# Products of two heads issued side by side on the column halves; the first attention's key remainder over 128 rows

## The chip, the cores and the metric

The program runs on one core of a Trainium2 chip. The metric is the device time of that core in microseconds (us), the median of several executions. Of the kernel before there are three: 2319.04, 2317.48 and 2319.41.

## The reference

Three transformer blocks follow each other on one sequence of 512 tokens with 1024 features, all in float32. The parts that the change touches, one in each block:

```python
# block 1: merged dilated attention, 8 heads of 64
s = jnp.einsum('bdhnqe,bdhnke->bdhnqk', qs, ks) * (E ** -0.5) + bias[None, None, :, None]
o = jnp.einsum('bdhnqk,bdhnke->bdhnqe', p, vs) / den
...
# block 2: attention, 8 heads, keys of 96, values of 64
s = jnp.einsum('bqhd,bkhd->bhqk', qi, k, preferred_element_type=jnp.float32) * scale
w = jax.nn.softmax(s, axis=-1).astype(v.dtype)
return jnp.einsum('bhqk,bkhd->bqhd', w, v)
...
# block 3: state space (SSD), 12 heads of 64, chunks of 128 tokens
cb = jnp.einsum('bclgn,bcsgn->bcgls', cc, bc)
y_diag = jnp.einsum('bcgls,bcghls,bcsghp->bclghp', cb, l_dec, xc)
y_off = jnp.einsum('bclgn,bcghpn,bcghl->bclghp', cc, prev, jnp.exp(a_cum))
```

Around them stand the projections of each block, a gated linear recurrence (block 1, after the attention), a long convolution (block 2), an mLSTM and a retention mixer (block 3), and two feed-forward layers.

## The kernel before

**Products.** A tile holds 128 features of all 512 tokens. A projection is a chain of products into one PSUM bank, three for each 128 rows of weights, since weights and activations are both split into a high and a low part (`acc_T`; the weights by L110 on ACT and L111 on DVE). Every product of the program is issued by `mm`, L116, so in the profile they all carry that line and are told apart by their tiles. A product named `128*64` in a row uses all 128 rows of TensorE's array and 64 of its columns: its result is 64 features of one head. Products whose operands are plain float32 go through the array in two passes, and a profile row counts passes (`x2` for one product); those of split parts take one.

**Banks.** The tiles of a tag go around a fixed number of banks: "mm" (projections) three, "s" (scores) two, "t" (transposes) two, "o" (values) one. A product into a tile waits until what the bank held before has been read.

**The order.** The program is written stage by stage, but the order on each engine is not the written one: a scheduler simulates the whole program (`schedule_with_timeline_sim=True`) and emits instructions by readiness and priority. Within an engine the emitted order is fixed; an instruction at the head that waits holds all behind it. Numbers behind a tile's name (mm_2236) count the tiles of the program as they are allocated, and order rows show them; profile rows leave them out.

**First attention** (`attn1`, four pairs of heads). A projected pair of q (or k) fills 128 partitions, 64 for each head. For head hh the tile q{hh} holds the high part of q in one half of its partitions and the low part in the other; k{hh} holds the high part of k in both. So one product over 128 rows gives q times the high part of k. The rest of k is `kl`: one tile for both heads, the half `kl[a]` for each, and its product with the high half of q uses 64 rows (`64*128` in a row). Each score block is written by these two products, 256 to 512 columns wide. DVE adds the bias and takes the maximum, ACT the exponential, POOL the division.

`values` goes through head 0 with its four blocks of keys, then head 1: for block j it transposes the 4 - j blocks of the probabilities p into a "t" bank (L599), copies them to SBUF (`pT`, two buffers, L604 on DVE for odd j, L606 on ACT for even), and multiplies v by pT, 512 - 128 j columns, into the 64 partitions of the head in bank "o". DVE's L609 (`of`) multiplies by the gate z, and ACT's L173 begins the split into the pair oa. Projections of the next pair and, after the last pair, of the recurrence stand between.

**Recurrence** (`hgrn`). For each head three projections, f, q and z, fill the three "mm" banks: L680 (`k`, tanh) and L681 (`b`, logarithm) read the first, L688 (`th`) the second, L693 (`th`) the third. Logarithms and tanh or exponentials need different tables, and ACT loads one at each switch (ACT_TABLE_LOAD). `decays` follows: differences `d` (POOL), their exponentials (ACT, L712), `qk` (DVE, L716), products `s<-qk` on TensorE, and `kd` (POOL, ACT, DVE, ending in L755), which is transposed at L760. Its tiles lie where those of the first attention were.

**Second attention** (eight heads). `scores` of a head gives four blocks P; `values(hd, ...)` transposes them (L1453), copies (`pT`, two buffers; L1456 on DVE for the last block, L1458 on ACT for the others) and multiplies, 512 columns each, into the head's half of "o". After block `SPREAD` = 1 of a second head the inverse row sums are spread over the partitions (`inverse_sums`). Output products of the convolution are held back to fill places in it.

**State space** (`Ssd`, called by `mix3`). For each of 12 heads, `decay` makes the decay factors (bank "o", DVE, ACT) and multiplies them with the shared products of B and C: `AD` inside the four chunks, `AO` between chunks, two buffers each. `values` then issues ten products of 128 columns into the head's half of "o", four of AD and six of AO, with `xd` (tokens times dt) as the other operand. The loop makes the decays of head hd + 1 before the values of head hd; a projection or two from `fill`, and the gate z of the next pair, stand between. `Retention` takes its AD and AO from the same pool.

At the end of block 1, eight tiles of x are loaded again by ACT's DMA queue (L840).

## Time and profile before

| | us |
| --- | --- |
| median of three executions | 2319.04 |
| span of the profiled execution | 2316.4 |
| TensorE (PE) busy in it | 2267.0 |
| DVE busy | 1389.2 |
| ACT busy | 941.6 |
| POOL busy | 537.1 |

The profiled execution is one of its own; the profile gives its span, and the time of the program lies around it. PE's rows show when a pass over the array starts and how long it lasted until its end; since passes are pipelined, one row's end overlaps the next one's start, and the pace is read from the starts. PEld is the loading of weights into the array, which runs beside it. In brackets behind a row stand the idle time before it and what ended that.

### The profile page before, as it was taken

How to read it: one execution, taken by the hardware profiler on the slowest of the kernel's cores; microseconds unless marked ns; L12 is line 12 of the kernel's file. 1: busy time of each engine (PE TensorE's matmuls, PEld its weight loads, DVE VectorE, ACT ScalarE, POOL GpSimd, SP SyncE). 2: the span in 40 equal slices, each digit the busy share in tenths (PEclk: the TensorE clock that was granted, in tenths of full speed). 3: DMA queues.
4: the chain of work that ended last, by engine and by line, in shares of the span. 5: the costliest groups of instructions: out<-in, count | busy, mean ns of one | idle time of the engine just before them, and what ended most of it. 6: DMA issues, size and time to landing. Idle time of an engine off the chain costs nothing.

```text
span 2316.4 us, 29278 instructions
## 1 busy us (share of the span) xinstructions
PE 2267.0 (98%) x11180; PEld 1837.4 (79%) x11180; DVE 1389.2 (60%) x2228; ACT 941.6 (41%) x1579; POOL 537.1 (23%) x457
## 2 busy tenths in 40 slices
PE   7899999999999999999999999999999999999998
PEld 3676798888888985678888887888887888888886
DVE  8754566663354597578637747876757665433333
ACT  4344455552243445644424424444444323322221
POOL 5232445541121135222101103000111211220220
PEclk7999999999999999999999999999999999999999
DMA  8542222124333342123232234212222322223222
GB/s 327 164 145 64 74 65 65 51 66 130 100 95 103 115 140 62 68 93 108 78 123 91 81 126 143 91 65 73 78 92 91 127 73 100 100 79 113 100 81 74
DMA packets 82163, 232.59 MB, mean 100 GB/s; under 512 B 10047, under 2 KB 10943, under 8 KB 82024
## 3 DMA queue, kind: packets, MB, share of 16 engines
q1 hardware_dynamic: 67208, 205.49, 26.9%
q10 hardware_dynamic: 14816, 25.25, 3.4%
q8 instruction: 88, 1.44, 0.2%
q14 instruction: 51, 0.42, 0.1%
HBM read 215.99 MB, written 15.22 MB: 100 GB/s over the span
## 4 chain that ended last, share of the span: by engine, by line
PE 57%; issue 2%; DVE 2%; ACT 1%; DMA 0%; POOL 0%; ACTq 0%; POOLq 0%; DVEq 0%
PE mm L116 48%; PE s L116 3%; PE o L116 3%; PE t L116 1%; PE t L1453 1%; DVE sg L1599 0%; DVE wl L111 0%; PE t L1422 0%; DMA x<-scr_x 0%; DVE x L2267 0%; DVE x L1600 0%; ACT P L1439 0%; ACT wh L110 0%; PE t L1953 0%; ACT A L182 0%
## 5 line engine op out<-in xcount | busy, mean ns | idle before, releaser
L116 PE MATMUL mm<-A,wh 128*128 128x512 f32 (+1 forms) x2192 | 692.6, 392 | 1.0 <-DVE A L183 1.0
L110 ACT CAST wh<-wr 128x1024 fp32r<-128x1024 f32 (+3 forms) x370 | 363.5, 984 | 653.9 <-PE mm L116 463.5
L111 DVE TENSOR_TENSOR wl<-wr,wh 128x1024 fp32r<-128x1024 f32 (+3 forms) x366 | 437.7, 1197 | 296.2 <-ACT wh L110 294.4
L116 PE MATMUL mm<-B,wh 128*128 128x512 f32 x1688 | 541.9, 397 | 3.2 <-DVE B L183 1.9
L116 PEld LDWEIGHTS mm<-A,wh 128*128 128x128 f32 (+1 forms) x2192 | 408.9, 187 | 88.2 <-DVE A L183 1.8
L116 PE MATMUL mm<-A,wl 128*128 128x512 f32 (+1 forms) x1096 | 429.0, 392 | 0.5 <-DVE wl L111 0.5
L116 PEld LDWEIGHTS mm<-B,wh 128*128 128x128 f32 x1688 | 316.4, 188 | 73.9 <-DVE B L183 2.9
L116 PE MATMUL mm<-B,wl 128*128 128x512 f32 x844 | 332.4, 394 | 0.1
L116 PEld LDWEIGHTS mm<-A,wl 128*128 128x128 f32 (+1 forms) x1096 | 205.2, 187 | 43.4 <-DVE wl L111 0.9
L116 PEld LDWEIGHTS mm<-B,wl 128*128 128x128 f32 x844 | 159.0, 188 | 34.5 <-issue 1.5
L116 PE MATMUL mm<-a,wh 128*128 128x512 f32 x448 | 140.4, 389 | 0.0
L222 POOL TENSOR_TENSOR r<-r,mhalf 128x4 f32<-128x4 f32 (+1 forms) x40 | 53.7, 1344 | 350.9 <-DVE r L221 350.9
L239 DVE TENSOR_TENSOR us<-mm,bc 128x512 f32<-128x512 f32 x95 | 65.2, 689 | 99.8 <-PE mm L116 99.0
L175 POOL TENSOR_TENSOR a<-sl,a 128x512 fp32r<-128x512 f32 x28 | 40.5, 1446 | 274.2 <-ACT a L173 274.2
L116 PEld LDWEIGHTS mm<-a,wh 128*128 128x128 f32 x448 | 84.1, 188 | 17.4
L116 PE MATMUL mm<-a,wl 128*128 128x512 f32 x224 | 86.8, 389 | 0.0
L116 PE MATMUL mm<-wh,A 128*128 128x256 f32 x448 | 85.4, 287 | 0.0
L116 PEld LDWEIGHTS mm<-wh,A 128*128 128x128 f32 x448 | 71.6, 193 | 2.4 <-issue 1.0
L2187 POOL TENSOR_TENSOR sl<-sl,bc 128x512 f32<-128x512 f32 x22 | 28.7, 1305 | 167.6 <-DVE sl L1545 167.6
L116 PE MATMUL mm<-wl,A 128*128 128x256 f32 x224 | 64.2, 287 | 1.0 <-DVE wl L111 1.0
L712 ACT ACTIVATE d<-d 128x512 f32<-128x512 f32 x56 | 35.2, 629 | 69.7 <-POOL d L711 69.7
L116 PE MATMUL mm<-wh,B 128*128 128x256 f32 x320 | 61.0, 288 | 0.0
(583 smaller groups left out, 3597.1 us busy)
## 6 DMA issues: line engine op xcount, KB each, us to landing
wr<-w2upg SPq DMA_DIRECT2D x22, 512.0 KB, 3.4
wr<-w2upu SPq DMA_DIRECT2D x22, 512.0 KB, 3.5
wr<-w3fg SPq DMA_DIRECT2D x22, 512.0 KB, 3.4
wr<-w3fu SPq DMA_DIRECT2D x22, 512.0 KB, 3.4
adar<-w1ada SPq DMA_DIRECT2D x32, 256.0 KB, 5.1
wr<-w3out SPq DMA_DIRECT2D x16, 512.0 KB, 3.4
wr<-w2uh SPq DMA_DIRECT2D x12, 512.0 KB, 3.6
wr<-w2dn SPq DMA_DIRECT2D x16, 384.0 KB, 2.9
```

The costliest lines, as they stand in the source:

```text
L110: nc.scalar.copy(out=hi[:, :n], in_=r[:, :n])
L111: (eng or nc.vector).tensor_tensor(out=lo[:, :n], in0=r[:, :n], in1=hi[:, :n].bitcast(F32), op=ALU.subtract)
L116: self.nc.tensor.matmul(out, a, b, start=start, stop=stop)
L175: eng.tensor_tensor(out=l[:p], in0=src, in1=hi[:p].bitcast(F32), op=ALU.subtract)
L222: nc.gpsimd.tensor_tensor(out=r, in0=r, in1=self.mhalf[:, :n], op=ALU.pow)
L239: self.nc.vector.tensor_tensor(out=out, in0=ps, in1=bc, op=ALU.mult)
L712: nc.scalar.activation(out=d, in_=d, func=AF.Exp)
L1453: nc.tensor.transpose(ps[:, i * P : (i + 1) * P], pt[i][:, j * P : (j + 1) * P], k.ident)
L2187: nc.gpsimd.tensor_tensor(out=s, in0=s, in1=norm.bc, op=ALU.mult)
```

## The change

- `mm` returns its instruction. A new method `together` issues a list of products at high priority, so that nothing comes between them, and makes the first depend on all the copies that the list needs.
- First attention: the remainder of k lies in two persistent tiles, kl0 and kl1, each zeroed once (POOL) and filled in its head's half, and the remainder product goes over all 128 rows. `values` has the blocks j outside and the two heads inside: both heads' transposes and copies (head 0's on ACT, head 1's on DVE, four pT buffers), then their two products by `together`.
- Second attention: the transposes and the copy of a block become `turn`, with six pT buffers. The first head of a pair makes its four pT and keeps them; the second head works in two groups, each of two blocks: its two turns, then four products, first and second head in turn, by `together`. The inverse sums come after the first group.
- State space: AD and AO have four buffers. `values` takes a pair and issues its 20 products in one list, the two heads in turn, after the last operation of both decays. The loop of `mix3` goes by pairs, with the decays of both heads of the next pair and its z ahead of the values.
- Two small tiles (lb, pss) are allocated wider than they are used, `dynamic_dma_scratch_size=2048` is given to the program, and comments are gone.

```diff
     def mm(self, out, a, b, start, stop):
-        self.nc.tensor.matmul(out, a, b, start=start, stop=stop)
+        return self.nc.tensor.matmul(out, a, b, start=start, stop=stop)
+
+    def together(self, mms, after):
+        info = mybir.DependencyInfo(mybir.DependencyClass.Sync, mybir.DependencyReason.DATA)
+        with self.tc.high_priority():
+            for i, args in enumerate(mms):
+                m = self.mm(*args)
+                if i == 0:
+                    for a in after:
+                        self.tc.add_manual_dep(m.ins, a.ins.name, info, reason="issued in a row")
...
 def attn1(k, h, tab, oa, op):
+        kls = [p.tile([P, T], F32R, tag=f"kl{hh}", name=f"kl{hh}") for hh in range(2)]
+        for t in kls:
+            nc.gpsimd.memset(t.bitcast(F32), 0.0)
...
-            kl = p.tile([P, T], F32R, tag="kl", bufs=1, name=k.name("kl"))
             for hh, (a, b) in enumerate(rows):
+                kl = kls[hh]
...
-                ks.append((kt, kl[a]))
+                ks.append((kt, kl))
...
-                    k.mm(ps[:, :m], q[hh][a, i * P : (i + 1) * P], kp[hh][1][:, :m], False, True)
+                    k.mm(ps[:, :m], q[hh][:, i * P : (i + 1) * P], kp[hh][1][:, :m], False, True)
...
             po = k.bank("o", 1)
-            for hh in range(2):
-                pt, off = pts[hh]
-                c0 = (pr % 2) * P + hh * 64
-                for j in range(NT):
-                    n = T - P * j
+            for j in range(NT):
+                n = T - P * j
+                es, ready = [], []
+                for hh in range(2):
+                    pt, off = pts[hh]
...
-                    e = p.tile([P, T], F32, tag="pT", bufs=2, name=k.name("pT"))
-                    if j % 2:
-                        nc.vector.tensor_copy(out=e[:, :n], in_=ps[:, :n])
+                    e = p.tile([P, T], F32, tag="pT", bufs=4, name=k.name("pT"))
+                    if hh:
+                        ready.append(nc.vector.tensor_copy(out=e[:, :n], in_=ps[:, :n]))
                     else:
-                        nc.scalar.copy(out=e[:, :n], in_=ps[:, :n])
-                    k.mm(po[hh * 64 : hh * 64 + 64, j * P :], v[:, j, c0 : c0 + 64], e[:, :n], j == 0, j == NT - 1)
+                        ready.append(nc.scalar.copy(out=e[:, :n], in_=ps[:, :n]))
+                    es.append(e)
+                mms = []
+                for hh, e in enumerate(es):
+                    c0 = (pr % 2) * P + hh * 64
+                    mms.append(
+                        (po[hh * 64 : hh * 64 + 64, j * P :], v[:, j, c0 : c0 + 64], e[:, :n], j == 0, j == NT - 1)
+                    )
+                k.together(mms, ready)
...
+            def turn(pt, j):
+                ps = k.bank("t", 2)
+                for i in range(NT):
+                    nc.tensor.transpose(ps[:, i * P : (i + 1) * P], pt[i][:, j * P : (j + 1) * P], k.ident)
+                e = pd.tile([P, T], F32, tag="pT", bufs=6, name=k.name("pT"))
+                return e, V.tensor_copy(out=e, in_=ps) if j == 3 else S.copy(out=e, in_=ps)
+
+            first = []
+
             def values(hd, pt, po, den):
                 hh = hd % 2
-                for j in range(NT):
...
-                    k.mm(po[hh * 64 : hh * 64 + 64], v[:, j, hd], e, j == 0, j == NT - 1)
-                    if hh and j == SPREAD:
+                if not hh:
+                    first[:] = [turn(pt, j) for j in range(NT)]
+                    return
+                for j0 in (0, 2):
+                    es = [(first[j], turn(pt, j)) for j in (j0, j0 + 1)]
+                    k.together(
+                        [
+                            (po[a * 64 : a * 64 + 64], v[:, j, hd - 1 + a], e[a][0], j == 0, j == NT - 1)
+                            for j, e in zip((j0, j0 + 1), es) for a in range(2)
+                        ],
+                        [e[a][1] for e in es for a in range(2)],
+                    )
+                    if j0 == 0:
                         rows = inverse_sums(den)
...
-        AD = pool.tile([P, NT, P], F32, tag="AD", bufs=2, name=k.name("AD"))
-        AO = pool.tile([P, 768], F32, tag="AO", bufs=2, name=k.name("AO"))
+        AD = pool.tile([P, NT, P], F32, tag="AD", bufs=4, name=k.name("AD"))
+        AO = pool.tile([P, 768], F32, tag="AO", bufs=4, name=k.name("AO"))
...
-    def values(self, hd, AD, AO, po):
+    def values(self, pr, As, po):
         k, xd = self.k, self.xd
-        hh = hd % 2
-        out = po[hh * 64 : hh * 64 + 64]
+        mms = []
         for c in range(NT):
             sl = slice(c * P, (c + 1) * P)
-            for a in range(c):
-                o = OFF[a, c]
-                k.mm(out[:, sl], xd[:, a, hd * 64 : hd * 64 + 64], AO[:, o : o + P], a == 0, False)
-            k.mm(out[:, sl], xd[:, c, hd * 64 : hd * 64 + 64], AD[:, c], c == 0, True)
+            for a in range(c + 1):
+                for hh, (AD, AO, _) in enumerate(As):
+                    x = xd[:, a, pr * P + hh * 64 : pr * P + hh * 64 + 64]
+                    d = AD[:, c] if a == c else AO[:, OFF[a, c] : OFF[a, c] + P]
+                    mms.append((po[hh * 64 : hh * 64 + 64, sl], x, d, a == 0, a == c))
+        k.together(mms, [A[2] for A in As])
...
-                A = s.decay(0)
-                po = None
-                for hd in range(12):
-                    if hd % 2 == 0:
-                        po, z = k.bank("o", 1), zn
-                    fill.pop(0)()
-                    nx = s.decay(hd + 1) if hd < 11 else None
-                    s.values(hd, *A, po)
-                    A = nx
-                    if hd % 2:
-                        s.end(hd // 2, po, z)
-                    elif hd < 10:
-                        zn = s.z(hd // 2 + 1)
+                As = [s.decay(0), s.decay(1)]
+                for pr in range(6):
+                    po, z = k.bank("o", 1), zn
+                    nx = []
+                    for j in range(2):
+                        fill.pop(0)()
+                        if pr < 5:
+                            nx.append(s.decay(2 * pr + 2 + j))
+                    if pr < 5:
+                        zn = s.z(pr + 1)
+                    s.values(pr, As, po)
+                    As = nx
+                    s.end(pr, po, z)
```

Where this moves instructions, in the order that each kernel's build gives. First TensorE in the state space of before, at the last products of a pair: AD_12667 and AO_12668 are the first head's decays, AD_12751 and AO_12752 the second's, and o_12701 is their bank.

```order
L116 MATMUL o_12701<-AD_12667,xd 64x128
L116 MATMUL o_12701<-AO_12668,xd 64x128 x3
L116 MATMUL o_12701<-AD_12667,xd 64x128
L116 MATMUL o_12701<-AD_12751,xd 64x128
L116 MATMUL o_12701<-AO_12752,xd 64x128
L116 MATMUL o_12701<-AD_12751,xd 64x128
L116 MATMUL o_12701<-AO_12752,xd 64x128 x2
```

And of the change, at the first products of a pair (AD_12432 and AO_12433 belong to the first head, AD_12454 and AO_12455 to the second; mm_12995 is a projection):

```order
L116 MATMUL mm_12995<-wh_13004,B_11862 128x256
L116 MATMUL o_12474<-AD_12432,xd 64x128
L116 MATMUL o_12474<-AD_12454,xd 64x128
L116 MATMUL o_12474<-AO_12433,xd 64x128
L116 MATMUL o_12474<-AO_12455,xd 64x128
L116 MATMUL o_12474<-AD_12432,xd 64x128
L116 MATMUL o_12474<-AD_12454,xd 64x128
```

Before, each head's ten products stood together and the second head's followed the first's; now the two alternate.

Next TensorE at the end of the first attention, where the last products by values (o_1975, pT) stand among the projections of the recurrence's first head (mm_2164 f, mm_2201 q, mm_2236 z; mm_2392 is f of its second head). Before:

```order
L116 MATMUL mm_2236<-A_605,wh_2239 128x512
L116 MATMUL mm_2236<-A_605,wl_2240 128x512
L116 MATMUL mm_2236<-A_606,wh_2239 128x512
L116 MATMUL o_1975<-pT_2020,v_1395 64x256
L116 MATMUL o_1975<-pT_2025,v_1395 64x128
L116 MATMUL mm_2236<-A_609,wh_2239 128x512
L116 MATMUL mm_2236<-A_609,wl_2240 128x512
```

Of the change:

```order
L116 MATMUL o_1975<-pT_1988,v_1396 64x512
L612 MATMUL t_2006<-ident,p_1849 128x128 x2
L116 MATMUL o_1975<-pT_1996,v_1396 64x384
L116 MATMUL o_1975<-pT_2002,v_1396 64x384
L612 MATMUL t_2011<-ident,p_1892 128x128 x2
L612 MATMUL t_2018<-ident,p_1849 128x128
L612 MATMUL t_2022<-ident,p_1892 128x128
L116 MATMUL o_1975<-pT_2009,v_1396 64x256
L116 MATMUL o_1975<-pT_2014,v_1396 64x256
L116 MATMUL o_1975<-pT_2020,v_1396 64x128
L116 MATMUL o_1975<-pT_2024,v_1396 64x128
L116 MATMUL mm_2392<-A_601,wh_2395 128x512
```

Before, 18 products of mm_2236 follow the last product by values, then 24 of mm_2392, 24 of mm_2429 and 2 of mm_2464, and then the recurrence's first s<-qk. In the change all of mm_2236 comes earlier; the 24 of mm_2392 and 6 of mm_2429 stand between the last product by values and that s<-qk.

Last ACT at the same boundary, where the recurrence starts (k_2195, th_2232, b_2196 and th_2267 are of its first head, k_2423 of its second). Before:

```order
L680 ACTIVATE k_2195<-mm_2164 128x512
L688 ACTIVATE th_2232<-mm_2201 128x512
L110 CAST wh_2467<-wr_2465 128x1024
L681 ACT_TABLE_LOAD
L681 ACTIVATE b_2196<-k_2195,lb 128x512
L693 ACT_TABLE_LOAD
L693 ACTIVATE th_2267<-mm_2236 128x512
```

Of the change, whose lines stand 22 further down:

```order
L702 ACTIVATE k_2195<-mm_2164 128x512
L710 ACTIVATE th_2232<-mm_2201 128x512
L862 DMA x_4687<-xT 128x512
L862 DMA x_4689<-xT 128x512
L703 ACT_TABLE_LOAD
L703 ACTIVATE b_2196<-k_2195,lb 128x512
L862 DMA x_4691<-xT 128x512
L862 DMA x_4693<-xT 128x512
L715 ACT_TABLE_LOAD
L715 ACTIVATE th_2267<-mm_2236 128x512
```

The loads of x, which the program of before issues much later, now stand among the recurrence's first operations on ACT, and a cast of wh no longer stands ahead of the first logarithm.

## The prediction

> **What bounds the kernel now.** I read the page's busy shares first, then its chain, then the busy time in the stretches that the change touches.

> ```profile
> span 2316.4 us, 29278 instructions
> PE 2267.0 (98%) x11180; PEld 1837.4 (79%) x11180; DVE 1389.2 (60%) x2228; ACT 941.6 (41%) x1579; POOL 537.1 (23%) x457
> PE 57%; issue 2%; DVE 2%; ACT 1%; DMA 0%; POOL 0%; ACTq 0%; POOLq 0%; DVEq 0%
> 118.00:256.80 138.80, 138.80 (x677) 99.26 (x676) 67.16 (x189) 57.89 (x123) 34.88 (x32) 1.00 0.31 96
> 876.00:918.00 42.00, 39.24 (x169) 20.52 (x170) 35.65 (x51) 28.09 (x60) 26.30 (x18) 1.00 0.21 63
> 1500.00:1650.00 150.00, 150.00 (x929) 127.89 (x928) 106.36 (x231) 67.66 (x147) 11.27 (x6) 1.00 0.21 71
> ```

> TensorE (PE) is busy 98% of the span, and no other engine has more than 2% of the chain. The stretches (columns: length, then busy PE, PEld, DVE, ACT, POOL, then clock and DMA) are first attention, the front third of second attention, and the state-space heads. In the first and last PE never rests and DVE has 48% and 71%: a microsecond taken off PE there is a microsecond off the span, until PE is made to wait. The middle one differs: DVE is at 85%.

> **What the products cost now.** The products by values and state-space heads write 64 partitions each. Their PE time, by stretch:

> ```profile
> 118.00:256.80 138.80, 22.31 (x64) 1.00 0.31 96
> 870.00:1000.00 130.00, 34.09 (x64) 1.00 0.22 69
> 1480.00:1660.00 180.00, 26.39 (x240) 1.00 0.21 71
> ```

> Together 82.8 us. Each product is two passes over the array (64 passes for the 32 products of either attention). What one costs alone, with its borders, stands in the timeline (start, length):

> ```profile
> 906.46 0.39 PE L116 MATMUL s<-kT,qT 96*128 96x512 f32 x1
> 906.78 1.07 PE L116 MATMUL o<-pT,v 128*64 128x512 f32 x2
> 907.78 0.66 PE L1453 MATMUL t<-ident,P 128*128 128x128 f32 x4
> ...
> 1617.98 0.39 PE L116 MATMUL mm<-B,wl 128*128 128x512 f32 x1
> 1618.21 0.39 PE L116 MATMUL mm<-B,wh 128*128 128x512 f32 x1
> 1618.52 0.43 PE L116 MATMUL o<-AD,xd 128*64 128x128 f32 x2
> ...
> 1622.65 0.50 PE L116 MATMUL mm<-B,wh 128*128 128x512 f32 x1
> ```

> Lengths overlap, so I read starts. A projection follows the next after 0.23; the first 128*64 product comes 0.31 after one, so changing the shape of the array costs about 0.09 going in, and as much going out. Of the 1.00 from 906.78 to 907.78, two passes take 0.43 each (512 columns at 1.2 per ns), a first weight load 0.05, and the way out 0.09. So a run of these products costs 0.24 plus its passes. The 40 passes of this state-space pair take 4.13; but for the accident shown next they start 0.109 apart (128 columns at the same rate).

> **Do two halves run at once?** The program of before has one accident that answers this: where the second head of a state-space pair follows the first without a break.

> ```profile
> 1548.31 0.71 PE L116 MATMUL o<-AO,xd 128*64 128x128 f32 x5
> 1548.75 0.32 PE L116 MATMUL o<-AD,xd 128*64 128x128 f32 x1
> 1548.85 0.27 PE L116 MATMUL o<-AO,xd 128*64 128x128 f32 x1
> 1548.91 0.32 PE L116 MATMUL o<-AD,xd 128*64 128x128 f32 x2
> 1549.02 0.27 PE L116 MATMUL o<-AO,xd 128*64 128x128 f32 x1
> 1549.07 0.27 PE L116 MATMUL o<-AD,xd 128*64 128x128 f32 x1
> 1549.13 0.27 PE L116 MATMUL o<-AO,xd 128*64 128x128 f32 x1
> ```

> From 1548.85 to 1549.13 six passes start, 0.055 apart: twice the usual pace. By the order of before (first fence of the section on the change) the first head still had AO and AD passes to go when the AD of the second began at 1548.75. So the second half of the array takes work past waiting work of the first, and two heads issued in turn should take half. For 512 columns no row shows it; the bounds are no overlap and 2x, and I take 2x: a projection moves 512 columns in 0.23, so two of these passes in 0.43 ask no more columns per ns than that.

> [...]

> **Gains, term by term.**
> - First attention: 16 runs of one pair (4 pairs of heads, 4 blocks). Passes of a pair side by side: 2 x (0.43 + 0.32 + 0.21 + 0.11) = 2.13, with 4 x 0.24 = 3.1; four pairs 12.4, from 22.3: **9.9**.
> - Second attention: 8 runs of two pairs, 0.24 + 4 x 0.43 = 1.96 each, 15.7 from 34.1: **18.4**.
> - State space: 6 runs of 40 passes, 0.24 + 40 x 0.0545 = 2.4 each, 14.5 from 26.4: **11.9**.
> - The remainder of the keys (kl) over 128 rows:

> ```profile
> 174.22 0.36 PE L116 MATMUL s<-k,q 128*128 128x256 f32 x1
> 174.52 0.38 PE L116 MATMUL s<-kl,q 64*128 64x256 f32 x1
> 174.83 0.38 PE L116 MATMUL s<-k,q 128*128 128x256 f32 x1
> 175.14 0.38 PE L116 MATMUL s<-kl,q 64*128 64x256 f32 x1
> 175.45 0.50 PE L116 MATMUL mm<-A,wh 128*128 128x512 f32 x1
> ```

> Four products of 256 columns take 1.23, 0.31 each; at the projections' pace they need 0.12 each, 0.48. The difference, 0.75, is the change of shape at both borders of each kl, and with 128 rows it goes. 32 kl products, two to a group: 16 x 0.75 = **12.0**, with 0 as the other end, should the shape not be what costs it.

> Sum of gains **52.2**.

> **What comes late.** (a) The end of first attention. In the order of before 18 projections of mm_2236 stand behind the last product by values, and 50 more before the first s<-qk of the recurrence; in the new order none of mm_2236, 30 in all. The recurrence starts only when first attention is over, since ACT's k follows its cast of oa:

> ```profile
> 255.99 0.86 PE L116 MATMUL o<-pT,v 128*64 128x256 f32 x4
> 256.96 0.68 DVE L609 SCALAR_TENSOR_TENSOR of<-o,z 128x512 f32<-128x512 f32 x1
> ...
> 260.14 0.60 ACT L680 ACTIVATE k<-mm 128x512 f32<-128x512 f32 x1 [1.84 <-DVE hog L803]
> ...
> 269.68 0.58 ACT L680 ACTIVATE k<-mm 128x512 f32<-128x512 f32 x1
> ...
> 273.86 1.28 ACT L712 ACT_TABLE_LOAD   x1
> ...
> 277.23 0.96 DVE L755 TENSOR_TENSOR kd<-kd,k 128x384 f32<-128x384 f32 x1
> 274.67 1.10 PE L116 MATMUL s<-qk 128*128 128x64 f32 x8 [0.41 <-DVE qk L716]
> 278.25 0.55 PE L760 MATMUL t<-ident,kd 128*128 128x128 f32 x3 [1.49 <-DVE kd L755]
> ```

> With F for the start of DVE's of (256.96), k ends at F + 3.8 and kd at F + 21.2. Of the three "mm" banks mm_2164, mm_2201 and mm_2236 hold all, and mm_2392 needs the one that k empties: PE, done with the values at F - 0.1, now waits 3.9 there. Up to the transposes of kd it has 30 projections (6.8) and 8 small products (1.1), so it could be there at F + 7.8 without the wait, or F + 11.7 with it. When is kd ready? In the new order ACT does kd's inputs ahead of the next head's k, a logarithm, a cast and two table loads (269.68 to 275.14 in before): with one d (0.63) of that stretch still needed, 4.8 earlier, F + 16.4. Against that six x loads now stand in ACT's queue there, eight of which took 4.02 to issue (last row of the next fence) beside its operations; I add 0.9. So kd is ready at F + 17.3, and PE waits 9.5 in all, where before had 0.41 + 1.49: **7.6 lost**. Bounds: 3.9, the bank alone, and 11.5, kd at F + 21.2.

> (b) The last two blocks there have their transposes, copies and products back to back; a copy takes 0.59 on ACT:

> ```profile
> L1458 ACT COPY pT<-t x24: 559/586/595, 877.2 to 991.0; 128x512 f32<-128x512 f32 x24
> L116 PE MATMUL o<-pT,v 128*64 128x512 f32 x27 | 14.6, 618 | 0.4 <-ACT pT L1458 0.4
> 286.00:290.00 4.00, 4.00 (x22) 3.91 (x23) 3.93 (x11) 1.77 (x4) 2.60 (x4) 0.61 0.00 0
> 520.40 4.02 ACTq L840 DMA_DIRECT2D x<-xT  x8
> ```

> Two to three copies in the open: **1.3** (0 to 2.8). Everywhere else of the two attentions several projections or score products stand between the last transpose and the run that needs it, more than a copy.

> (c) Front of second attention: its 27 passes (second row) are 13.5 products, 14.7 us with borders, which become 13.5 / 4 x 1.96 = 6.6. PE would need 42 - 8.1 = 33.9, less than DVE's 35.65. With DVE at 95% the stretch takes 37.5, so **3.6 lost** (1.8 to 6).

> (d) The clock: the waits at 274 to 286 were followed by a stretch at half clock (0.61 from 286 to 290, third row). More idle time may bring another: **1.0** (0 to 1.7). (e) Small waits at other runs, of which the 27 passes had 0.4 (second row of the last fence): **1.4** (0 to 5).

> At nothing: two memsets on POOL (23% busy); copies shifted from ACT to DVE (DVE half idle there); the eight x loads, which leave 520 (last row) for the recurrence's start, beyond what (a) holds, as issues run beside ACT's operations; 19 weight loads on SP that follow the moved z products, four buffers ahead with DMA at 21%. If that cover fails, a late load costs PE its delay once.

> Losses 14.9, net **37.3**. The profiled span 2316.4 becomes 2279.1; the median of the runs, 2319.04, is 2.6 longer than that span, so the time is **2281.7**.

> **Rivals.**
> 1. Nearly all the gain arrives: kd early, DVE's work shifted behind the front third, losses 5: 2272. For it: PE is 100% busy in two of the three stretches. Chance 20%.
> 2. Strict order: a half starts only behind the passes issued earlier. Then a pair takes 3 slots for 2, two pairs 5 for 4, 40 passes 21 for 20: gains 5.6 + 15.0 + 11.2 + 12.0 = 43.8, less 14.9: 2290. Against it, the AD at 1548.75 went past waiting passes; for it, no row has 512 columns. Chance 12%. [...]
> 3. No overlap (the change doesn't do what it says): only borders are saved, 1.3 + 4.7 - 1.2, and kl, 16.8 in all; losses (a) and (b) 8.9, while (c) goes: 2311. The passes 0.055 apart speak against it. Chance 5%. [...]
> 4. Slower: a run waits for the copies of both heads, and all of PE's queue waits behind it. There are 24 such runs in the attentions. If the last copy comes d after PE arrives, the kernel loses 24 d + 8.9 against 52.2: break-even at d = 1.8, three copies of 0.59; at four copies, 2.4, it is 14 slower, 2333. Against it: the projections between, named in (b). Chance 3%.
> 5. My forecast, waits between 10 and 20: 2277 to 2287. Chance 60%.

> So faster by over 0.2% (about what a measurement of this kernel can tell from no change) 0.95, within it 0.02, slower 0.03. The range holds rivals 1 and 2 and the bounds of the losses, and leaves out 3 and 4: 2268 to 2296.

> **What would show it.** The products by values and state space at 12, 16 and 15 us of PE time by stretch; two starts within 0.1 of each other in each run; kl as 128*128 starting 0.12 to 0.23 after its k; PE idle for 4 at the first mm after first attention and for some 6 more up to the transposes of kd; DVE near 95% in the front of second attention. Wrong would be: 512-column passes of the two halves 0.43 apart, or new waits of over 20 in sum.

## The result

Four executions of the changed kernel took 2282.62 us in the median (2279.68 to 2287.6), four of before beside them 2319.22: a ratio of 0.9844, 95% interval 0.9825 to 0.9863. The forecast was 2281.7. (Of the runs below one execution, in experiment 4, took 2767.35 at a granted clock of 0.748; it is left out of that median.) The page of the profiled execution (whole span, busy time of the engines, chain that ended last):

```profile
span 2278.5 us, 29275 instructions
PE 2216.6 (97%) x11180; PEld 1822.6 (80%) x11180; DVE 1391.8 (61%) x2228; ACT 939.0 (41%) x1579; POOL 534.1 (23%) x459
PE 56%; DVE 2%; issue 2%; ACT 1%; POOL 0%; POOLq 0%; DVEq 0%; ACTq 0%
```

TensorE is busy 50.4 us less and idle 61.9 us of the span instead of 49.4, 12.5 more. Where that happened is seen by cutting both spans at the same instructions: the first s<-k of first attention, the last transposes of kd in the recurrence, the second wait at the start of the feed-forward layer of block 2, and the last transposes of the program. Busy time by such a stage (columns: length, then busy PE, PEld, DVE, ACT, POOL, clock, DMA), before:

```profile
109.49:498.31 388.82, 384.50 (x2219) 316.25 (x2218) 238.75 (x482) 193.10 (x357) 166.82 (x184) 1.00 0.25 78
498.31:1027.50 529.19, 521.37 (x2539) 407.09 (x2537) 306.18 (x435) 230.23 (x397) 136.55 (x107) 1.00 0.32 101
1027.50:2306.76 1279.26, 1273.56 (x6087) 1056.58 (x6087) 752.91 (x1198) 470.82 (x753) 188.71 (x130) 1.00 0.28 93
```

and after:

```profile
109.46:481.42 371.96, 362.86 (x2218) 310.93 (x2217) 239.05 (x483) 191.51 (x357) 166.74 (x184) 0.99 0.28 87
481.42:1001.57 520.15, 504.60 (x2539) 408.80 (x2537) 307.62 (x434) 229.57 (x397) 135.76 (x107) 0.99 0.31 99
1001.57:2268.75 1267.18, 1261.38 (x6086) 1045.19 (x6087) 754.21 (x1198) 470.41 (x753) 186.12 (x130) 1.00 0.29 94
```

The stage of first attention and recurrence is 16.9 shorter, that of second attention 9.0, the rest with the state space 12.1. Length less busy time is TensorE's idle time: 4.3 became 9.1, 7.8 became 15.6, and in the rest it stayed at 5.7 to 5.8.

What the products that write one half of the columns cost, by the same view as before (PE busy in them, first attention, second attention, state space):

```profile
104.80:241.10 136.30, 11.95 (x64) 1.00 0.41 126
868.00:994.00 126.00, 15.82 (x64) 0.96 0.25 82
1480.00:1620.00 140.00, 14.43 (x240) 1.00 0.23 76
```

So 10.4, 18.3 and 12.0 less, against 9.9, 18.4 and 11.9 in the forecast. Four products of the scores in first attention, and one run of a pair there, on the timeline (start, length):

```profile
109.46 0.28 PE L116 MATMUL s<-k,q 128*128 128x256 f32 x1
109.58 0.28 PE L116 MATMUL s<-kl,q 128*128 128x256 f32 x1
109.70 0.28 PE L116 MATMUL s<-k,q 128*128 128x256 f32 x1
109.82 0.28 PE L116 MATMUL s<-kl,q 128*128 128x256 f32 x1
109.94 0.40 PE L116 MATMUL mm<-A,wh 128*128 128x512 f32 x1
...
148.53 1.08 PE L116 MATMUL o<-pT,v 128*64 128x512 f32 x4
149.54 0.66 PE L612 MATMUL t<-ident,p 128*128 128x128 f32 x4
```

Four passes of 512 columns take 1.01 with their borders (148.53 to 149.54), where two took 1.00: both halves run at once. By the trace the four start at 148.53, 148.54, 149.01 and 149.02. The four score products take 0.48, as forecast, instead of 1.23.

The end of first attention, on the timeline (the last column is the idle time before and its releaser). F, the start of DVE's of, is 241.07:

```profile
241.07 0.69 DVE L630 SCALAR_TENSOR_TENSOR of<-o,z 128x512 f32<-128x512 f32 x1 [0.54 <-PE o L116]
...
244.85 0.80 PE L116 MATMUL mm<-A,wh 128*128 128x512 f32 x1 [3.82 <-ACT k L702]
...
256.67 0.58 DVE L777 TENSOR_TENSOR kd<-kd,k 128x384 f32<-128x384 f32 x1 [0.31 <-ACT kd L776]
257.30 0.55 PE L782 MATMUL t<-ident,kd 128*128 128x128 f32 x3 [1.67 <-DVE kd L777]
```

The wait for k's bank came as forecast, 3.8. kd was ready at F + 16.2, and TensorE waited 1.7 for it. In second attention the waits (engine, line, releaser: us, times, longest) are led by

```profile
PE s L116 <- ACT P L1461: 6.3, 6, 3.3
```

and the longest of them has this on DVE:

```profile
879.16 0.67 DVE L1389 TENSOR_TENSOR tmp<-tmp,tmp 128x512 f32<-128x512 f32 x1
...
882.65 1.77 DVE L193 SCALAR_TENSOR_TENSOR B<-ya,vec,B 128x512 fp32r<-128x512 f32 x1
884.34 1.75 DVE L1389 TENSOR_TENSOR tmp<-tmp,tmp 128x512 f32<-128x512 f32 x1
886.01 1.27 DVE L1459 TENSOR_REDUCE st<-s 128x1 f32<-128x512 f32 x2
...
887.56 0.79 PE L116 MATMUL s<-kT,qT 96*128 96x512 f32 x1 [3.34 <-ACT P L1461]
```

The maxima st of two score blocks, whose last products started between 882.17 and 883.18, stand in DVE's order behind work of the convolution (L1389) and the split of the attention's own output (B); ACT's exponential P follows st, and TensorE needs the bank that P empties.

### The profile page after: what moved, and what is told of

Read it like the earlier page. It is cut to its first block, busy times and chain, and to the rows that moved or that the text cites. A ratio compares the mean times of both kernels' runs of the same rounds, so it can differ in the third digit from the quotient of the medians.

```text
span 2278.5 us, 29275 instructions
## 1 busy us (share of the span) xinstructions
PE 2216.6 (97%) x11180; PEld 1822.6 (80%) x11180; DVE 1391.8 (61%) x2228; ACT 939.0 (41%) x1579; POOL 534.1 (23%) x459
## 4 chain that ended last, share of the span: by engine, by line
PE 56%; DVE 2%; issue 2%; ACT 1%; POOL 0%; POOLq 0%; DVEq 0%; ACTq 0%
PE mm L116 49%; PE s L116 3%; PE o L116 2%; PE t L116 1%; DVE sg L1634 0%; PE t L1474 0%; ACT wh L110 0%; DVE wl L111 0%; DVE x L2304 0%; DVE B L193 0%; DVE x L1635 0%; DVE st L1459 0%; PE t L1989 0%; ACT A L192 0%; PE t L1952 0%
## 5 line engine op out<-in xcount | busy, mean ns | idle before, releaser
L116 PE MATMUL mm<-A,wh 128*128 128x512 f32 (+1 forms) x2192 | 693.2, 392 | 4.8 <-ACT k L702 3.8
L111 DVE TENSOR_TENSOR wl<-wr,wh 128x1024 fp32r<-128x1024 f32 (+3 forms) x366 | 438.0, 1198 | 282.4 <-ACT wh L110 280.4
L116 PE MATMUL mm<-B,wh 128*128 128x512 f32 x1688 | 541.9, 397 | 3.6 <-DVE B L193 2.1
L116 PEld LDWEIGHTS mm<-A,wh 128*128 128x128 f32 (+1 forms) x2192 | 409.8, 188 | 91.0 <-ACT k L702 4.1
L116 PE MATMUL mm<-A,wl 128*128 128x512 f32 (+1 forms) x1096 | 430.1, 393 | 1.1 <-DVE wl L111 1.1
L116 PEld LDWEIGHTS mm<-B,wh 128*128 128x128 f32 x1688 | 316.6, 188 | 75.4 <-DVE B L193 3.7
L116 PE MATMUL mm<-B,wl 128*128 128x512 f32 x844 | 332.4, 394 | 0.0
L116 PEld LDWEIGHTS mm<-A,wl 128*128 128x128 f32 (+1 forms) x1096 | 206.0, 188 | 44.0 <-DVE wl L111 1.9
L116 PEld LDWEIGHTS mm<-B,wl 128*128 128x128 f32 x844 | 159.0, 188 | 34.0 <-issue 1.2
L116 PE MATMUL mm<-a,wh 128*128 128x512 f32 x448 | 140.4, 389 | 0.0
L116 PEld LDWEIGHTS mm<-a,wh 128*128 128x128 f32 x448 | 84.1, 188 | 17.4
L116 PE MATMUL mm<-a,wl 128*128 128x512 f32 x224 | 86.8, 389 | 0.0
L116 PE MATMUL mm<-wh,A 128*128 128x256 f32 x448 | 84.6, 285 | 0.0
L116 PEld LDWEIGHTS mm<-wh,A 128*128 128x128 f32 x448 | 70.7, 191 | 1.1 <-issue 0.6
L116 PE MATMUL mm<-wl,A 128*128 128x256 f32 x224 | 63.7, 285 | 1.0 <-DVE wl L111 1.0
L1609 DVE TENSOR_TENSOR x<-x,mm 128x512 f32<-128x512 f32 x32 | 22.0, 687 | 64.5 <-PE mm L116 64.5
```

The lines of the kernel that those rows point to most:

```text
L111: (eng or nc.vector).tensor_tensor(out=lo[:, :n], in0=r[:, :n], in1=hi[:, :n].bitcast(F32), op=ALU.subtract)
L116: return self.nc.tensor.matmul(out, a, b, start=start, stop=stop)
L1609: k.nc.vector.tensor_tensor(out=xs[n], in0=xs[n], in1=ps, op=ALU.add)
```

## The experiments

All but the first change the changed kernel; times are medians, stages as above.

**1. The remainder of the keys alone, in the kernel before.**

```diff
+        kls = [p.tile([P, T], F32R, tag=f"kl{hh}", name=f"kl{hh}") for hh in range(2)]
...
-                    k.mm(ps[:, :m], q[hh][a, i * P : (i + 1) * P], kp[hh][1][:, :m], False, True)
+                    k.mm(ps[:, :m], q[hh][:, i * P : (i + 1) * P], kp[hh][1][:, :m], False, True)
```

> The kernel before with the remainder of the keys over 128 rows alone (two zeroed tiles, nothing else of the change). Theory (the change of the array's shape at both borders is what the 64-row products cost): each of the 32 costs its columns alone, 0.12 for 256, and the time falls by 10 to 12, to 2307 to 2309; TensorE's order at the end of first attention stays that of before, so no wait of 3.9 for a bank appears there. Rival (they cost it by something else): 0, 2319.

The two tiles are zeroed once; the edit also has the change's `dynamic_dma_scratch_size`. Measured 2308.94 against 2319.84, ratio 0.9957 (0.9942 to 0.9972): 10.9 less, the theory's time. Its first stage, and a row in it that before does not have:

```profile
108.73:490.91 382.18, 374.21 (x2219) 315.62 (x2218) 238.47 (x483) 193.04 (x357) 167.96 (x184) 0.99 0.28 86
```

```profile
118.65 0.50 PE L116 MATMUL mm<-A,wl 128*128 128x512 f32 x1 [3.60 <-DVE wl L111]
```

TensorE is busy 10.3 less (384.50 less 374.21), although it ran 3.4 us more at half clock than before (the mean granted clock is 0.99 in this row and 1.00 in that of before), and in this execution 3.6 of the gain were handed to a new wait: the low part of a weight, made by DVE, is late. It is in the changed kernel too (0.5 in its profile). Experiments 7 and 10 follow it.

**2. How far past waiting passes a pass can start.** Inside a run, the heads change after g products instead of after each:

```diff
+        hs = mms[0::2], mms[1::2]
+        mms = [m for c in range(0, len(hs[0]), g) for h in hs for m in h[c : c + g]]
```

> The changed kernel with the products inside a run grouped by head, nothing else: the six state-space pairs change heads after 1, 2, 3, 4, 5 and 10 products of a head (10 is head after head); in second attention pairs 1 and 3 change after every product, pairs 2 and 4 after two. It tells how far a pass may stand behind waiting ones and still start on the free half. In the kernel before, head after head, 40 passes cost 4.22 with borders where 40 x 0.109 + 0.24 would be 4.60, so 3.4 passes were saved at the one change of heads. Theory (a pass starts when its half is free and it is among the 4 oldest that have not started): 2.42, 2.53, 2.75, 3.18, 3.62 and 4.27 us for the six pairs; in second attention 1.96 alternating and 2.39 by twos. Rival (a depth of 8 or more): 2.42, 2.42, 2.42, 2.53, 2.75, 3.84, and 1.96 for both. Rival (the two halves need the two products next to each other): 2.42, 3.5, 3.8 and more. TensorE never rests around the state space, so the time grows by the sum of the differences: theory 4.4 + 0.9 = some 5 us, to 2287.

The six state-space pairs (length of the window, PE busy in their 40 passes), for g = 1, 2, 3, 4, 5 and 10:

```profile
1509.00:1513.00 4.00, 2.40 (x40) 1.00 0.00 0
1531.00:1535.00 4.00, 2.45 (x40) 1.00 0.01 4
1550.00:1554.00 4.00, 2.67 (x40) 1.00 0.22 60
1573.00:1577.20 4.20, 3.00 (x40) 1.00 0.00 0
1600.00:1604.00 4.00, 3.44 (x40) 1.00 0.43 138
1609.00:1615.00 6.00, 4.20 (x40) 1.00 0.26 90
```

The expected numbers hold borders that this view counts some 0.03 shorter. With the 0.03, 2.43, 2.48, 2.70, 3.03, 3.47 and 4.23 lie between the depth of 4 and one of 5 (2.42, 2.42, 2.64, 2.86, 3.29 and 4.16 by the same reckoning), and far from both rivals. The twos in second attention speak for 5: their runs take as long as those that alternate, where a depth of 4 would give 2.39 and one of 5 gives 1.96. The second run of the second pair, in twos (all eight runs last 1.94):

```profile
908.11 1.94 PE L116 MATMUL o<-pT,v 128*64 128x512 f32 x8
```

A pass goes past three to four that were issued before it and haven't started (one of these starts beside it), and alternating after each product isn't needed: after every second product the halves run side by side nearly as well; head after head, only the one change of heads is saved, as in before. The time was 2287.25 in the one execution, 4.6 above the change, where 5 were expected; as executions of the change differ by more than that, only the windows tell.

**3. A space of its own for the recurrence's first k, b, th and q.**

(The same for b, th and q.)

```diff
-            kk = p.tile([P, T], F32, tag="k", bufs=2, name=k.name("k"))
+            kk = (p if hd else op).tile([P, T], F32, tag="k" if hd else "k0", bufs=2 if hd else 1, name=k.name("k"))
...
```

> The changed kernel, but k, b, th and q of the recurrence's first head lie in a space of their own instead of that of the first attention, so that they need not wait for its end; the scheduler then emits mm_2392 and mm_2429 ahead of the last products by values. Theory (the wait of 3.8 at the first product after first attention, and the half clock from 242.4 to 249.2 that comes with it, are there because k must wait for the cast of oa): TensorE goes on without a wait, no half clock there, kd's wait of 1.7 stays within 0 to 3; gain 3.8 + about 2 (4.4 of busy time at half clock) = 4 to 7, to 2276 to 2279. Rival (what sets the pace there is kd, with the chain of POOL, ACT and DVE that starts when first attention ends): the wait moves to the transposes of kd, 5 to 7 long, gain under 2.

Measured 2284.42 (2281.12 to 2285.99): no gain, the theory's time missed. TensorE went on with the two banks that came free, and met the same wait at the third, whose gate z still lies in the space of the recurrence:

```profile
256.92 0.50 PE L116 MATMUL mm<-A,wh 128*128 128x512 f32 x1 [3.38 <-DVE z L717]
```

The first stage stayed at 372.6. No wait was left at kd, so the rival's place was wrong too. A bank emptied earlier didn't help here; that TensorE only spent the time on work that it then lacked at the boundary is the reading that experiments 5, 8 and 10 test.

**4. The convolution's second forward half held back to the fourth head.**

```diff
-            for f in fill:
-                f()
+            for i, f in enumerate(fill):
+                with k.tc.issue_after(marks[9]) if i == 3 else ExitStack():
+                    f()
```

> The changed kernel, but the second half of the convolution's forward transform, which fills places in second attention, is held back until the scores of the fourth head. Theory (second attention keeps only 9.1 of its gain of some 18, since in the first four heads DVE has 97% busy with the work of both, its maxima come late, TensorE waits 3.3 for ACT's exponentials and then runs 10.2 at half clock): the wait of 3.3 goes, DVE falls below 95% there, and the time falls by 4 to 8, to 2275 to 2279. Rival (DVE's work is only moved to the next heads, which then wait as long): within 2 of 2282.6. Second rival (the runs by values, which wait for the copies of both heads, lose it): no change of the sum of waits.

Measured 2288.43 in three executions, 5.8 slower than the change. The longest wait for P fell from 3.3 to 1.6, but DVE was now full from 895 to 915 (19.27 of 20, where the change has 14.00), and idle time of the stage rose to 16.7 (527.07 less 510.41):

```profile
483.22:1010.29 527.07, 510.41 (x2538) 411.56 (x2536) 308.50 (x435) 230.17 (x397) 134.88 (x107) 0.98 0.31 97
```

```profile
895.00:915.00 20.00, 16.58 (x85) 9.21 (x84) 19.27 (x24) 13.29 (x29) 13.47 (x10) 0.99 0.27 79
```

That is the rival, and worse: 20.5 us of this stage ran at half clock (a mean of 0.98 in its row), where the profiled change had 10.2 (0.99). Whether DVE is the cause, moving its work could not show; experiments 6 and 9 take it away.

**5. The gate of the recurrence's first head held back until first attention is over.**

```diff
+            k.hold = k.last_pe()
...
-            ps = k.proj_T([k.aps["w1zb"][hd]], h)
+            with ExitStack() if hd else k.tc.issue_after(k.hold):
+                ps = k.proj_T([k.aps["w1zb"][hd]], h)
```

> The changed kernel, but the projection of the gate z of the recurrence's first head (mm_2236, 24 products, 5.5 us) is held back until the last product by values of first attention has been issued; in the new order 24 + 24 + 14 projections stand between that product and the recurrence's first s<-qk. The run with tiles of their own has shown that freeing a bank earlier only lets TensorE run further ahead, until the banks are full again when the recurrence's start comes. Theory (what is lost there is that no work is left for TensorE until k and kd are ready, 3.8 and 16.2 us after the last DVE operation of first attention): no wait of 3.8, no half clock between 242 and 250 (6.8 at half clock, about 0.38 each by the two profiles that differ in it, 2.6), no wait of 1.7 at kd; against it copies of the last two blocks in the open, 3 x 0.6. Gain 3.8 + 1.7 + 2.6 - 1.8 = 6, to 2275 to 2280. Rival (the waits move to the copies of the last values, now without filler): gain under 2. By the stages of the profile: from the first s<-k to the last transposes of kd 372.2 becomes 366 by the theory, 370 or more by the rival.

Measured 2281.39 (2278.69 to 2284.32). The wait of 3.8 is gone and kd's is 1.0, while 2.3 appeared at the copies of the last blocks:

```profile
235.48 0.55 PE L612 MATMUL t<-ident,p 128*128 128x128 f32 x3 [1.01 <-ACT pT L619]
236.96 1.98 PE L116 MATMUL o<-pT,v 128*64 128x512 f32 x4 [0.93 <-DVE pT L617]
...
241.58 0.33 PE L612 MATMUL t<-ident,p 128*128 128x128 f32 x1 [0.35 <-ACT pT L619]
...
242.66 0.50 PE L116 MATMUL mm<-A,wh 128*128 128x512 f32 x1
```

The stage still took 372.3, as this execution had 3.4 at the weight of experiment 1, near 120 us. By itself the run decides nothing; with that wait away (experiment 10) the gain is there.

**6. Three copies of second attention on ACT instead of DVE.**

```diff
-                return e, V.tensor_copy(out=e, in_=ps) if j == 3 else S.copy(out=e, in_=ps)
+                return e, V.tensor_copy(out=e, in_=ps) if j == 3 and len(ya) > 1 else S.copy(out=e, in_=ps)
```

> The changed kernel, but the three copies pT that DVE makes in the second attention's first heads are made by ACT. Theory (in the first four heads the pace is DVE's: 44 of 47 us busy): DVE is 3 x 0.68 = 2.0 less busy, TensorE's idle time in the stage of second attention falls from 15.0 to 13, the stage shortens by 1 to 3 (the half clock adds or takes up to 3 by itself, so idle time is what tells). Rival (the pace is that of the chain of each score block, product to maximum to exponential over two banks, and ACT is on it): idle 15 or more. Time by the theory 2279 to 2282, by the rival 2283 or more.

Measured 2286.45 (2283.05 to 2291.02), idle time of the stage 14.8 instead of 15.6 (the 15.0 of the expectation is 15.6 by the stage used here): between the two. TensorE's waits for P fell from 6.3 to 1.6, and waits for ACT's copies (2.7) and for a split on ACT (2.9) took their place. The profiled execution is the slowest of the four, with 27.3 us of the stage at half clock (a mean of 0.97 in the stage; the execution has 0.982, the change's profiled one 0.986). Inconclusive on DVE; on ACT the copies only made other waits.

**7. The gate loads of first attention from POOL's queue instead of SP's.**

```diff
-            k.nc.sync.dma_start(out=self.r[kk][j], in_=k.aps["w1ada"]...
+            (k.nc.gpsimd if self.part == 2 else k.nc.sync).dma_start(out=self.r[kk][j], in_=k.aps["w1ada"]...
```

> The changed kernel, but the loads of w_ada's third part, which first attention consumes on the side (adar, 16 of 256 KB), are issued from POOL's queue instead of SP's. In every profile of a kernel with the new remainder product TensorE waits at 116 to 120 us for the low part of a weight, 0.5, 3.6, 2.2, 2.5, 3.4 and 1.6 long, where the kernel before does not: the load of w1k is issued at 114.7 in before, and at 116.3 to 119.7 in these, behind five adar loads that SP issues in 8.7 to 11.8 us, while TensorE comes there earlier. Theory (the load stands behind the adar loads in SP's order, and the faster products have used up its cover): w1k is issued by 112, the wait is gone, no half clock near 120, time 1 to 4 less than 2282.6. Rival (it is the DMA engines' rate, 63 to 90% busy there, whatever the queue): the wait stays within 0.5 to 3.6, time within 1.5.

Measured 2282.49 (2278.8 to 2285.34): nothing; the wait is 1.2 here, and w1k was issued at 117.2, no earlier. The theory fell, and with it the load as a cause: TensorE's wait here is for a weight that had been loaded before. DVE's timeline of experiment 1, where the wait is longest, shows what makes wl late:

```profile
113.28 1.42 DVE L415 SCALAR_TENSOR_TENSOR ada<-adar,silc,ada 128x512 f32<-128x512 f32 x2 [2.88 <-DMA adar<-w1ada]
116.71 0.75 DVE L415 SCALAR_TENSOR_TENSOR ada<-adar,silc,ada 128x512 f32<-128x512 f32 x1 [2.02 <-DMA adar<-w1ada]
117.38 1.22 DVE L111 TENSOR_TENSOR wl<-wr,wh 128x1024 fp32r<-128x1024 f32 x1
```

wl stands in DVE's order behind steps of ada, which wait for their adar loads; with POOL's queue it is the same (2.79 at 115.32). There are only two adar tiles, so a load starts when a step has freed one.

**8. Experiments 5 and 7 together.**

> Both the gate loads from POOL's queue and the projection of the recurrence's first gate held back. Theory (both waits are separate): the stage from the first s<-k to the last transposes of kd takes 366 to 369, time 2276 to 2280. Rival (one of them is no wait of its own): as the better of the two alone, 2281.

Measured 2279.76 (2276.75 to 2282.59), first stage 368.7: the time expected. The wait for wl did not occur in this profile, but as it varies between executions (0.2 to 3.6 in those of the other kernels), this is no proof that the queue helps.

**9. Second attention without the convolution's spectral products.** In both forward halves the products of the spectra, on DVE and POOL, are left out, so that the convolution is not the reference's; the attention is whole.

```diff
...
-                    V.tensor_tensor(out=t, in0=a, in1=k0, op=ALU.mult)
-                    V.tensor_tensor(out=k0, in0=b, in1=k0, op=ALU.mult)
-                    G.tensor_tensor(out=a, in0=a, in1=k1, op=ALU.mult)
-                    V.tensor_tensor(out=b, in0=b, in1=k1, op=ALU.mult)
-                    G.tensor_tensor(out=t, in0=t, in1=b, op=ALU.subtract)
-                    G.tensor_tensor(out=a, in0=a, in1=k0, op=ALU.add)
-                    m.append((t, a))
+                    m.append((k1, a))
```

> The changed kernel without the products of the two spectra in the convolution's forward transform: six operations on DVE and six on POOL in each of its two halves are left out, so that the output is not the reference's; what remains of it, and all of the attention, stays. Copies moved from DVE to ACT only changed which wait it was (idle time of the stage 14.2 against 15.0). Theory (in the first four heads DVE sets the pace, 44 of 47 us busy, and POOL slows it, 1.75 for an operation of 0.67): with some 11 us of DVE's work gone, idle time of TensorE in the stage falls from 15.0 to 7 to 10, the wait of 3.3 and the half clock go. Rival (the chain of each score block, from product to maximum to exponential to transpose to copy over two banks, sets it now that TensorE has 20 us less to do): idle time 12 or more.

Each of these six operations runs for both parts of the spectrum. Measured 2275.3 (2273.4 to 2280.35). The stage, and the 51 us from its first scores on, here and in the changed kernel:

```profile
480.65:993.84 513.19, 502.57 (x2538) 407.61 (x2536) 294.93 (x422) 229.14 (x397) 120.38 (x95) 0.99 0.32 100
...
844.00:895.00 51.00, 47.73 (x270) 36.70 (x269) 44.15 (x61) 34.97 (x68) 19.02 (x13) 0.93 0.46 147
```

```profile
844.00:895.00 51.00, 41.39 (x200) 28.49 (x199) 47.56 (x63) 31.47 (x67) 28.17 (x20) 0.93 0.30 89
```

Idle time of the stage falls from 15.6 to 10.6, the wait of 3.3 is gone, and in the same 51 us TensorE does 270 passes instead of 200. The other half of the expectation failed: the clock of these 51 us is 0.93 in both; a wait of 2.4 for P now stands in the first scores, followed by 6.8 us at half clock:

```profile
852.38 1.37 PE L116 MATMUL s<-kT,qT 96*128 96x512 f32 x3 [2.39 <-ACT P L1454]
```

So 4.9 us of idle time go with the elementwise work on DVE and POOL, against the 7.7 that the change had added in this stage; 10.6 is just above the range expected. How much the kernel before would lose without that work wasn't run, so the 4.9 need not all belong to the 7.7. Nor does the run part the two ways in which it can act: maxima that come sooner, and independent products that are ready sooner (the first mm<-wh,A at 860.68, in the change at 873.11).

**10. Six adar tiles instead of two, and the gate held back as in 5.**

```diff
-        gate = Ada(k, p, 2, lambda kk: [p.tile([P, T], F32, tag="adar", bufs=2, ...
+        gate = Ada(k, p, 2, lambda kk: [p.tile([P, T], F32, tag="adar", bufs=6, ...
```

> The changed kernel with six adar buffers instead of two (issued by SP as before), and with the projection of the recurrence's first gate held back as in the fifth run. The seventh run moved the queue and left the wait at 117 us, and its profile names what held it: DVE makes the low part of the weight (wl, L111) only after three to four steps of ada, and each of these waits 0.8 to 4.7 for its adar load, as only two tiles are there. Theory (the loads are too shallow, and the faster products have used up the cover of 0 that before just had): the ada steps run without waits at 105 to 115, wl is ready before TensorE comes, no wait over 0.3 between 110 and 125; stage from the first s<-k to the last transposes of kd 366 to 368.5, time 2276 to 2279. Rival (the DMA engines cannot bring them sooner): wait 0.5 to 3.5 as before, time 2279 to 2282.

Measured 2276.4 (2275.73 to 2278.75), ratio to before 0.9817 (0.9803 to 0.9831); beside it the change stands at 2282.55 (experiment 11). DVE's ada steps run on, TensorE doesn't wait for wl, and the stage is within the expected 366 to 368.5:

```profile
110.11 2.28 DVE L425 SCALAR_TENSOR_TENSOR ada<-adar,silc,ada 128x512 f32<-128x512 f32 x3
112.31 1.22 DVE L111 TENSOR_TENSOR wl<-wr,wh 128x1024 fp32r<-128x1024 f32 x1
```

```profile
109.39:476.16 366.77, 361.81 (x2218) 309.99 (x2217) 240.75 (x481) 191.82 (x358) 168.67 (x184) 1.00 0.29 87
```

Both waits of the first stage are gone (but 1.0 at kd and 2.3 at the copies), and this is the fastest version of the whole computation here, 6.2 below the change and 43.0 below before. (The intervals of 10 and of the change still touch; seven of the change's eight executions are slower than the slowest of 10.) What the six tiles bring by themselves was not run: the wait for wl was missing in experiment 8 too, with two tiles. That the steps of ada no longer wait ahead of wl is what this profile adds.

**11. The change once more.**

> The changed kernel once more, on the same chip and beside the same runs of before, for the spread of its time and its stages: 2279 to 2288; first attention and recurrence 372 to 374, second attention 517 to 522 by how much of it falls into a half clock.

Measured 2282.55 (2277.2 to 2285.87), ratio 0.9839 (0.9825 to 0.9853). Its second stage against that of the first profile:

```profile
481.56:998.82 517.26, 501.58 (x2539) 406.96 (x2537) 306.41 (x434) 229.27 (x397) 137.03 (x107) 1.00 0.32 99
```

Idle time is the same, 15.7 and 15.6, and so is the longest wait for P, 3.3, yet the stage is 2.9 shorter: TensorE ran 3.4 us at half clock here and 10.2 there (last section). That is 2.9 / 6.8 = 0.42 us for a microsecond at half clock, and accounts for nearly all of the 3.1 between the two spans (2275.4, 2278.5).

## Why the prediction was right

The time was right to 0.9 us, the sum of the terms partly because errors cancelled.

- **Two halves at once: right.** 512 columns behave as the accident with 128 columns did. Strict order (rival 2) would have left runs of 3 and 5 slots; the rows show 2 and 4. The gains 9.9, 18.4, 11.9 came as 10.4, 18.3, 12.0. A start only behind the passes issued earlier is not what was measured: experiment 2 has the second head start past three to four passes of the first that were issued earlier. The weight loads did not keep the halves apart (rival 3): both heads' products use all 128 rows, and all four loads of the run at 148.53 are done within 0.20 of its start, beside its first two passes, which take 0.48.
- **The remainder: right in cause, a little large.** 12.0 forecast; the kernel with nothing else gained 10.9, and TensorE 10.3 of busy time, or some 11.7 without its 3.4 more at half clock. The sum had no term for what came with it: faster products reached a weight part that had just been in time, and waited 0.2 to 3.6 for it, or not at all, depending on the execution. It wasn't the weight's load (experiment 7); the steps of ada ahead of it on DVE are what the rows show, and in experiment 10 both their waits and this one are gone.
- **(a) The boundary: right in kind, too large.** 3.9 for the bank came as 3.8; for kd 5.6 more were forecast and 1.7 came. kd was ready at F + 16.2 instead of 17.3, near the 16.4 that stood before 0.9 was added for the x loads, and TensorE came late itself: at F + 14.6 (257.30 less 1.67 less 241.07) instead of F + 11.7, as its 30 projections took 9.1 instead of 6.8, 4.4 us of them at half clock, and the small products 1.7 instead of 1.1. So part of the missing wait is in the clock's term. The copies of (b), 1.3, came as 0.4.
- **(c), (e) Second attention: too small.** 3.6 and 1.4 were put down; idle time grew by 7.7. The step that failed is "with DVE at 95% the stretch takes 37.5": a stretch of the order of before says how much DVE has to do, not that a maximum will stand behind 3.4 us of other work just when two banks are full. That idle time hangs on DVE's and POOL's work, experiment 9 shows, for 4.9 us; the rest stays open.
- **(d) The clock: mis-sized.** 1.0 (0 to 1.7) was put down, with the boundary in mind; in the profiled execution 6.8 and 10.2 us ran at half clock in the two stages where before had 3.4 and 0, (17.1 - 3.4) x 0.42 = 5.7, and 2.9 in experiment 11. The same waits thus cost nearly 3 us more in one execution than in another. Over the eight executions of the change, which differ by 10 us, the time goes roughly with the mean granted clock (2277.2 at 0.988, 2287.6 at 0.981); that the clock is the reason in all of them is not shown.
- **State space: right.** 12.1 for 11.9, idle time unchanged; the z products ahead of the values and their weight loads cost nothing.
- **The sum.** First stage forecast too little (21.9 less 7.6 and shares of (b), (d): some 12; 16.9 came), second too much (18.4 less 5 and shares: some 13; 9.0 came). The two errors, +5 and -4, cancelled. The terms as measured don't add up either: gains of 10.4 + 11.7 + 18.3 + 12.0 = 52.4, less 12.5 of idle time and 5.7 of clock, make 34.2, where the span fell by 37.9. So 3.7 more was saved, 2.7 of it in second attention, and no run shows where. Rivals 1 and 4 did not come: idle time grew by 12.5 and not by 5, and copies waited for cost 1.2 in second attention and 0.4 in first.

## What to carry to other kernels

Products that use half of the array's columns are worth pairing wherever their operands can be ready together; issuing them a product or two apart is near enough (40 passes took 2.40 us one by one and 2.45 in twos, experiment 2). Once such products are short, what they used to hide comes out: look at what is queued ahead of each small operation on which the tensor engine waits, and count an idle stretch like those of 2.4 to 3.8 us here twice, once as a wait and once for the clock after it (3.4 to 10.2 us at half clock went with these in the profiles of the change and of experiments 9 and 11). Where two stages meet, try to hold back independent work for the gap before clearing the way for it to run earlier: here the first shortened the stage from 372.0 to 368.7 and 366.8 (experiments 8 and 10, which both change the side loads too), and the second didn't (experiment 3, 372.6).

## What the runs showed of the hardware

```profile
242.00:243.00 1.00, 0.00 (x0) 0.00 (x0) 0.55 (x1) 0.41 (x1) 0.00 (x0) 0.70 0.00 0
249.00:250.00 1.00, 1.00 (x6) 0.79 (x5) 0.65 (x2) 0.84 (x2) 1.00 (x3) 0.88 1.03 395
...
887.00:888.00 1.00, 0.44 (x1) 0.44 (x2) 1.00 (x3) 1.00 (x4) 0.92 (x2) 0.76 0.00 0
897.00:898.00 1.00, 1.00 (x5) 0.41 (x6) 0.82 (x3) 0.72 (x2) 0.00 (x0) 0.62 0.00 0
```

The first pair: 0.30 missing in the window is 0.60 at half clock, so from 242.40 to 249.24, 6.84. The second, around the wait of 3.3 in second attention: from 887.52 to 897.76, 10.24. In before, in the stretch that the prediction quotes, it is 3.4. In these the fall comes during a wait or just behind it and lasts on into the work that follows; how long differs between executions, 10.2 and 3.4 behind the same wait of 3.3 (experiment 11). In experiment 9 a wait of 2.4 stands ahead of 6.8 us at half clock. The pair of profiles in experiment 11 gives 0.42 us lost for a microsecond at half clock.

An elementwise operation of DVE can take 2.6 times as long: L1389 took 0.67 at 879.16 and 1.75 at 884.34, where an operation of POOL ran beside it. That POOL is the cause was not tried by itself, and it is not so every time: L1391 took its 0.67 at 880.37 beside a POOL operation (L1393, 2.19 there and 1.27 at 886.24).
